# The mixture's weights two steps later in branch A's head loop, and the mixture in three places of a step

## The chip, the cores and the metric

The kernel runs on one core of one Trainium2 chip. The metric is the device time of one execution in microseconds (us). The core has five engines that run side by side, each in the order of its own instructions: PE (TensorE, matmuls), DVE (VectorE), ACT (ScalarE), POOL (GpSimd) and SP (SyncE, which here only issues DMAs). They wait for each other by semaphores, which the tile framework places. An engine whose next instruction waits does nothing of what stands behind it.

## The reference

One encoder layer over 1280 rows (1024 of a sample, 256 of a prompt) of width 1024: RMS norm, one wide projection, two attention branches side by side, gates, an output projection, an MLP with squared ReLU, a final norm. The branches are what matters here.

```python
o_a, _ = _banded_attention(qa, ka, va, A_WINDOW, 1, rel_bias[:, :A_HEADS], sink)
o_b = _dilated_mixture(qb, kb, vb, rel_bias[:, A_HEADS:])
merged = gates[:, :, 0] * (o_a.reshape(b, S, A_Q) @ w_branch_a) + gates[:, :, 1] * (o_b @ w_branch_b)
```

Branch A has 8 heads with a window of 128. Branch B has three groups of 4 heads with dilations 1, 4 and 16. Each group gives an output and, for every row and head, the log-sum-exp of its logits. The mixture weighs the three groups:

```python
alpha = jax.nn.softmax(jnp.stack(lses), axis=0)
o = jnp.sum(alpha[..., None] * jnp.stack(outs).astype(jnp.float32), axis=0)
```

## The kernel before

The kernel goes through its stages one after the other: norm and values, projections with branch B's attention beside the last of them, branch A's attention (about 552 to 710 us of the profile), gates and output projection, MLP up, MLP down. Float32 products are made of three matmuls of split operands (high and low parts), so PE is busy nearly all the time. In the stages that matter here the order of each engine's instructions is the order in which the Python code issues them; no scheduler changes it. Buffers come from pools: the pool `w` has 10 of 4 KB a partition, and the mixture's tiles `r`, the split weights `whi` and `wlo`, raw weights and the gate logits `gs` all come from it.

**The head loop** (lines 1336 to 1371). Branch A's heads are taken two at a time (a head pair u of 4), and each pair has 10 tiles of 128 rows. The list `order` holds the 40 (u, t). One step of the loop takes two tiles, so j runs over 0, 2, ..., 40, and the stages of a tile are spread over steps. In a step j stand, in this order:

1. scores of tile j on PE (L1093, L1094); DVE adds the bias and takes the maximum (L1095), and makes the negated maximum (`nm_a`, L1099); a piece of the fill; exponentials on ACT (L1105);
2. values of the tiles j-4 and j-3 on PE (L1132), the output copy on DVE (L1135, called the output copy in what follows) and its store by POOL's DMA queue (L1136);
3. **first place of the mixture** (L1345); a piece of the fill;
4. transposes of tile j-2's probabilities on PE (L1117), copied out of PSUM by ACT (L273) and, where the tile has three blocks, also by DVE (L275);
5. scores of tile j+1 and a piece of the fill;
6. transposes of tile j-1 with their copies; **second place of the mixture** (L1357); exponentials of tile j+1.

PE's *fill* is the generator `logits` (L1146): the gates' plain projections, cut into pieces of 4 or 8 matmuls. For each new column block the loop also splits a weight tile (ACT L231, DVE L235). At the steps with t = 0, SP loads the next head pair's queries (and keys for every second pair) and POOL loads its bias (L458), behind the step's other work.

**The mixture** is the generator `merge` (L1175). A call `next(merges)` runs it to its next `yield`. It holds:

- ahead of the loop: the maxima and sums of branch B (`nm_b`, `l_b`) are turned by PE, copied by DVE (L1182), written to DRAM by 13 small DMAs of POOL's queue (`scr_n`, L1187) and read back in another arrangement by 12 (L1204);
- first call in the loop: DVE copies the re-read parts into one order (L1209), takes the minimum over the groups and the differences (L1214 to L1216); ACT takes the exponential (L1217);
- second call: DVE sums, inverts and multiplies (L1219 to L1232), POOL's queue stores the weights (`scr_c`, 6 DMAs, L1235);
- third call: the load of item 0;
- then 18 items (three column blocks, two head pairs, three groups), two calls each: one loads the next item (`r`: branch B's outputs, L1250, and the weights spread over 64 partitions, two DMAs, L1253, all of POOL's queue) and multiplies this one on POOL (L1267); the other adds the product to `merged` on DVE (L1271), which groups 1 and 2 need and group 0 does not.

With two places a step from step 4 on, the first call comes behind the output copy of step 4, the second at the end of step 4, the products of items 0, 1, 2, ... at the ends of steps 6, 8, 10, ..., and each add at the output copy two steps later. The last item is left for `run(merges)` behind the loop (L1375). `merged` of the first column block is read in step 36 (`high_b`, `low_b`).

The functions that the diff touches, with the lines of the profile:

Of the kernel before, what the change touches and what calls it, by code (L numbers as in the profile page):

```python
# [97 lines left out]
def encoder_kernel(  # L98
# [120 lines left out]
    def fetch():  # L219
        src, shape, _ = specs[len(raws)]  # L220
        raws.append(wslot("raw", shape))
        nc.sync.dma_start(raws[-1], src)
# [200 lines left out]
    def load_unit(u):  # L423

        st = {}
        g = u // 2
        if u == 0:
            shared["kp"] = slot("kp", (P, 4, NP), F32R)
        if u % 2 == 0:
            kk = [slot("kk", (P, NS), F32R) for _ in range(2)]  # L430
            for i in range(2):
                for r in HALVES:
                    nc.sync.dma_start(kk[i][r, :].bitcast(F32), scr_ka[g, i, :, :NS])
                    nc.sync.dma_start(shared["kp"][r, 2 * g + i, :].bitcast(F32), scr_ka[g, i, :, NS:])
            shared["k"] = [Pair(kk[i], shared["kp"][:, 2 * g + i, :]) for i in range(2)]
        st["q"] = [Pair(slot("q", (P, NS), F32R), None) for _ in range(2)]
        for h in range(2):
            nc.sync.dma_start(st["q"][h].s.bitcast(F32), scr_qa[u][h].rearrange("a d t -> (a d) t")[:, :NS])
        if u:
            load_prompt(u, st)  # L440
        else:
            shared["v"] = [slot("va", (P, 8, P)), None]
            nc.sync.dma_start(shared["v"][0],
                              scr_v[:NS, 512 : 512 + P].rearrange("(t p) c -> p t c", p=P))
        st["k"], st["v"] = shared["k"], shared["v"]
        return st
# [9 lines left out]
    def load_bias(u, make):  # L456
        b = make("bias", (P, 2, 3 * P))
        nc.gpsimd.dma_start(b, toeplitz(0, 3 * P, -P, 2 * u))  # L458
        return b
# [611 lines left out]
    if True:  # L1071
# [3 lines left out]
        def a3(name, shape=(P, 2, 3 * P), n=3, dt=F32):  # L1075
            return att.tile(list(shape), dt, name=name, tag=name, bufs=n)
# [8 lines left out]
        def scores(u, t):  # L1085
            st, bias = units[u]
            lo, W, c0 = tiles[t]
            s = a3("s", n=3)
            m = small.tile([P, 2], F32, name="m", tag="m")
            for h in range(2):  # L1090
                ps = bank("sc")
                q = st["q"][h][:, P * t : P * t + P]
                nc.tensor.matmul(ps[:, :W], q, st["k"][1][:, P * lo : P * lo + W], start=True, stop=False)  # L1093
                nc.tensor.matmul(ps[:, :W], q, st["k"][0][:, P * lo : P * lo + W], start=False, stop=True)  # L1094
                nc.vector.tensor_tensor_reduce(  # L1095
                    s[:, h, :W], ps[:, :W], bias[:, h, c0 : c0 + W], 1.0, -3.0e38,
                    op0=ALU.add, op1=ALU.max, accum_out=m[:, h : h + 1],
                )
            nc.vector.scalar_tensor_tensor(nm_a[:, 2 * u : 2 * u + 2, t], m, -1.0, nsink[:, 2 * u : 2 * u + 2],  # L1099
                                           op0=ALU.mult, op1=ALU.min)  # L1100
            live[u, t] = s

        def exponential(u, t, h):
            W, s = tiles[t][1], live[u, t]
            nc.scalar.activation(s[:, h, :W], s[:, h, :W], AF.Exp, bias=nm_a[:, 2 * u + h : 2 * u + h + 1, t],  # L1105
                                 accum_out=l_a[:, 2 * u + h : 2 * u + h + 1, t])

        def transposes(u, t):

            W = tiles[t][1]  # L1110
            s = live[u, t]
            pt = a3("pt", (P, 6, P), 2)
            jobs = [(b, h) for b in range(W // P) for h in range(2)]
            for i, eng in ((0, nc.scalar), (4, nc.vector))[: 1 + (len(jobs) > 4)]:
                ps, e = bank("pt"), min(len(jobs), i + 4)
                for k, (b, h) in enumerate(jobs[i:e]):
                    nc.tensor.transpose(ps[:, P * k : P * k + P], s[:, h, P * b : P * b + P], ident)  # L1117
                moved(eng, pt[:, i:e, :], ps[:, : P * (e - i)].rearrange("p (i q) -> p i q", q=P))
            live[u, t] = pt

        def values_of(u, t):

            pv = bank("pv")
            for i in range(2):
                lo, W, _ = tiles[t + i]
                pt = live.pop((u, t + i))
                v, rest = units[u][0]["v"]
                for b in range(W // P):
                    k = lo + b
                    src = v[:, k, HALVES[u // 2]] if k < 8 else rest[:, k - 8, HALVES[u // 2]]  # L1130
                    for h in range(2):
                        nc.tensor.matmul(pv[HALVES[h], P * i : P * i + P], src, pt[:, 2 * b + h, :],  # L1132
                                         start=b == 0, stop=b == W // P - 1, skip_group_check=True)
            o = a3("o", (P, 2, P), 2)
            nc.vector.tensor_copy(o, pv[:, : 2 * P].rearrange("p (i q) -> p i q", i=2))  # L1135
            nc.gpsimd.dma_start(scr_o[t // 2][:, u], o)  # L1136
# [31 lines left out]
        def spread(src, g, b, x=0):  # L1168

            base, length, stride, R = place(g, b)  # L1170
            a = src[:, :]
            n = length // 32
            return bass.AP(a.tensor, a.offset + ROWS * P * x + base, [[n, P], [stride, R], [1, n]])

        def merge():  # L1175
# [23 lines left out]
            for g in range(3):  # L1199
                for b, sl in ((0, slice(0, 32)), (2, slice(32, 40))):  # L1200
                    R = place(g, b)[3]
                    for x in range(2):
                        dst = (raw[:, g, x, sl] if g else nat[:, x, 0, sl]).rearrange("p (r j) -> p r j", r=R)
                        nc.gpsimd.dma_start(dst, spread(scr_n, g, b, x))  # L1204
            yield
            for g in (1, 2):
                for b, sl in ((0, slice(0, 32)), (2, slice(32, 40))):
                    R = place(g, b)[3]
# [67 lines left out]
    if True:  # L1276
# [5 lines left out]
        def high_b(b):  # L1282

            ob_hi.block(b)
            ob_lo.block(b)
            nc.scalar.activation(ob_hi.t[b, 0], merged[b], AF.Copy)

        def low_b(b):
            nc.vector.tensor_tensor(ob_lo.t[b, 0], merged[b], ob_hi.t[b, 0].bitcast(F32), op=ALU.subtract)
# [3 lines left out]
        def load_o(t):  # L1293
            if t % 2 == 0:
                rows_o[t] = slot("o", (P, 4, 2, P))
                nc.sync.dma_start(rows_o[t], scr_o[t // 2])
# [34 lines left out]
        n = len(order)  # L1331
        fill = logits()
        merges = merge()
        next(merges)
        steps_of(fill, 2)
        for j in range(0, n + 2, 2):
            if j < n:
                scores(*order[j])
                next(fill)
                for h in range(2):  # L1340
                    exponential(*order[j], h)
            if j > 2:
                values_of(*order[j - 4])
                if j < n:
                    next(merges, None)  # L1345
            next(fill)
            if j:
                transposes(*order[j - 2])
            if j == n:
                next(fill)  # L1350
            if j < n:
                scores(*order[j + 1])
                next(fill)
            if j:
                transposes(*order[j - 1])
                if j > 2:
                    next(merges, None)  # L1357
            if j < n:
                for h in range(2):
                    exponential(*order[j + 1], h)  # L1360
            if j == n - 4:
                high_b(0)
                low_b(0)
            if j < n and order[j][1] == 0 and order[j][0] < 3:
                u = order[j][0] + 1
                units[u] = load_unit(u), load_bias(u, lambda name, shape: a3(name, shape, 2))
            if j in (n - 6, n - 4):
                fetch()
            if j == n - 2:
                load_o(0)  # L1370
                load_o(1)
# [573 lines left out]
```

## Time and profile before

| | us |
|---|---|
| median of 3 runs | 1724.98 |
| lowest and highest of the 3 | 1723.02, 1725.82 |
| the profiled execution | 1727.48 |
| its span, first to last instruction | 1725.3 |

The profile shows one execution. A row of a timeline has the start and the duration in us, the engine, the line, the operation, the tiles it writes and reads, the shapes and the count; in brackets stands how long the engine was idle ahead of it and what released it. DMA-issuing instructions stand on the engine that issues them, with the time of the issue; the landing comes later. A row of waits names who waited for whom, the total in us, how often, and the longest. A row of the windows gives a stretch, its length, the busy time (and number of instructions) of PE, PE's weight loads, DVE, ACT and POOL, then the granted clock of PE as a share of the full one, the DMA engines' share and GB/s.

### The profile page before, as it was taken

The page shows a single profiled execution, that of the slowest core. Times are in us where ns is not written, and L with a number is a line of the kernel's source. Part 1 is how long each engine was busy: PE and PEld are TensorE (multiplying, and loading weights), DVE is VectorE, ACT ScalarE, POOL GpSimd, SP SyncE. Part 2 cuts the span into 40 slices and gives each one's busy share as a digit, 9 for nine tenths or more (in the row PEclk, how much of TensorE's full clock was granted, in tenths as well). Part 3 has the DMA queues.
Part 4 walks back from the last instruction along what each step waited for, and adds up shares of the span by engine and source line. Part 5 has one row for each costly group of instructions (what it writes and reads, how often), then busy time and mean ns, then how long its engine had stood idle before and what let it go on. Part 6 is the DMA issues. An engine that isn't in the chain of part 4 may idle for free.

```text
span 1725.3 us, 24932 instructions
## 1 busy us (share of the span) xinstructions
PE 1682.3 (98%) x9230; PEld 1413.3 (82%) x9230; DVE 965.1 (56%) x1565; ACT 718.8 (42%) x1485; POOL 527.6 (31%) x451
## 2 busy tenths in 40 slices
PE   7999999999999799999999999999998999999998
PEld 6898888877778688888887888888887888888886
DVE  6733323445553466577368445454547776667575
ACT  6232222355553456654076333333334333333344
POOL 0212222212122664300100455555546242304140
PEclk9999999999999899999999999999999999999999
DMA  6414343576666574655021334433446835533333
GB/s 238 145 43 138 117 136 95 150 195 191 181 187 200 143 231 134 225 194 215 25 82 65 140 119 139 156 125 114 151 155 227 293 123 164 207 116 116 116 116 122
DMA packets 212424, 260.23 MB, mean 151 GB/s; under 512 B 21959, under 2 KB 141835, under 8 KB 212176
## 3 DMA queue, kind: packets, MB, share of 16 engines
q1 hardware_dynamic: 200704, 228.26, 40.1%
q0 software_dynamic: 10512, 28.29, 5.4%
q10 hardware_dynamic: 1088, 2.10, 0.4%
q8 instruction: 73, 1.20, 0.3%
q14 instruction: 47, 0.39, 0.1%
HBM read 173.03 MB, written 90.80 MB: 153 GB/s over the span
## 4 chain that ended last, share of the span: by engine, by line
PE 85%; issue 8%; DMA 2%; DVE 2%; POOL 1%; ACT 1%; SPq 0%; POOLq 0%; DVEq 0%; ACTq 0%
PE dn L355 21%; PE x L355 18%; PE mm L192 10%; PE z L355 9%; PE v L761 6%; PE mm L355 5%; PE pv L355 5%; PE y L355 4%; PE sc L538 2%; PE pv L581 1%; PE pt L568 1%; PE pv L1132 1%; DMA r<-scr_c 1%; PE pt L1117 1%; DMA scr_n<-cb 1%
## 5 line engine op out<-in xcount | busy, mean ns | idle before, releaser
L355 PE MATMUL dn<-dhi,ulo 128*128 128x512 f32 x448 | 175.3, 391 | 6.1 <-DVE ulo L186 6.1
L355 PE MATMUL dn<-dlo,uhi 128*128 128x512 f32 x448 | 175.0, 391 | 0.0
L355 PE MATMUL dn<-dhi,uhi 128*128 128x512 f32 x448 | 175.0, 391 | 0.0
L355 PE MATMUL x<-chi,wlo 128*128 128x512 f32 x424 | 167.6, 395 | 2.1 <-DVE u L1818 1.4
L355 PE MATMUL x<-clo,whi 128*128 128x512 f32 x424 | 165.8, 391 | 0.1
L355 PE MATMUL x<-chi,whi 128*128 128x512 f32 x424 | 165.1, 389 | 0.0
L322 DVE TENSOR_TENSOR wlo<-ta,whi 128x1024 fp32r<-128x1024 f32 x30 | 55.4, 1846 | 184.1 <-ACT whi L320 177.2
L322 DVE TENSOR_TENSOR wlo<-raw,whi 128x1024 fp32r<-128x1024 f32 x60 | 92.2, 1537 | 101.5 <-ACT whi L320 101.5
L397 POOL TENSOR_TENSOR tb<-raw 128x512 f32<-128x512 f32 x25 | 33.6, 1344 | 330.4 <-DMA raw<-in_w_in_dram 119.7
L355 PEld LDWEIGHTS dn<-dhi,ulo 128*128 128x128 f32 x448 | 84.6, 189 | 24.6 <-DVE ulo L186 7.0
L186 DVE TENSOR_TENSOR ulo<-uraw,uhi 128x1024 fp32r<-128x1024 f32 x56 | 93.9, 1695 | 13.5 <-ACT uhi L185 13.5
L355 PEld LDWEIGHTS dn<-dlo,uhi 128*128 128x128 f32 x448 | 84.5, 189 | 17.6
L355 PEld LDWEIGHTS dn<-dhi,uhi 128*128 128x128 f32 x448 | 84.5, 189 | 17.5
L355 PEld LDWEIGHTS x<-chi,wlo 128*128 128x128 f32 x424 | 79.7, 188 | 20.5 <-issue 3.1
L355 PEld LDWEIGHTS x<-chi,whi 128*128 128x128 f32 x424 | 79.6, 188 | 17.2
L355 PEld LDWEIGHTS x<-clo,whi 128*128 128x128 f32 x424 | 79.8, 188 | 14.8 <-DVE clo L322 0.4
L1643 POOL TENSOR_TENSOR t<-raw,t 128x1024 f32<-128x1024 f32 x16 | 45.4, 2854 | 149.5 <-DMA raw<-in_w_down_dram 138.6
L1794 DVE TENSOR_TENSOR v<-v,dn 128x512 f32<-128x512 f32 x90 | 59.6, 682 | 42.3 <-PE dn L355 41.3
L1890 POOL TENSOR_TENSOR u<-u,u 128x640 f32<-128x640 f32 x16 | 26.0, 1628 | 170.9 <-ACT u L1815 170.9
L558 ACT ACTIVATE s<-s,nm_b 128x128 f32<-128x128 f32 (+1 forms) x120 | 51.9, 434 | 54.5 <-DVE nm_b L550 54.5
L355 PE MATMUL pv<-phi,wlo 128*128 128x256 f32 x256 | 72.5, 283 | 1.7 <-ACT u L1814 1.7
L355 PE MATMUL dn<-dhi,up 128*128 128x512 f32 x224 | 73.5, 389 | 0.0
(312 smaller groups left out, 4676.3 us busy)
## 6 DMA issues: line engine op xcount, KB each, us to landing
scr_u<-u SPq DMA_DIRECT2D x112, 320.0 KB, 2.5
uraw<-scr_u SPq DMA_DIRECT2D x56, 512.0 KB, 4.0
raw<-in_w_in_dram SPq DMA_DIRECT2D x33, 512.0 KB, 5.5
raw<-in_w_up_dram SPq DMA_DIRECT2D x32, 512.0 KB, 4.8
raw<-in_w_down_dram SPq DMA_DIRECT2D x28, 512.0 KB, 6.3
sg<-scr_g SPq DMA_DIRECT2D x32, 256.0 KB, 5.9
uraw<-scr_u SPq DMA_DIRECT2D x28, 256.0 KB, 4.3
v<-scr_v SPq DMA_DIRECT2D x96, 64.0 KB, 2.5
```

The source lines that it names most:

```text
L186: nc.vector.tensor_tensor(lo, src, hi.bitcast(F32), op=ALU.subtract)
L192: nc.tensor.matmul(ps, a, b, start=i == 0, stop=i == len(seq) - 1)
L322: nc.vector.tensor_tensor(lo, src, hi.bitcast(F32), op=ALU.subtract)
L355: nc.tensor.matmul(ps, a, b, start=first and i == 0, stop=last and i == len(seq) - 1, skip_group_check=True)
L397: (nc.vector if vector else nc.gpsimd).tensor_tensor(o, x, y, op=ALU.subtract)
L538: nc.tensor.matmul(at(k, h)[p0 : p0 + nq, :], qk[rows, p0 : p0 + nq], qk[rows, P + P * a : P + P * a + W], start=True, stop=True, skip_gro ...
L558: nc.scalar.activation(s[:, h, :W], s[:, h, :W], AF.Exp, bias=nm[:, h : h + 1], accum_out=l[:, h : h + 1])
L568: nc.tensor.transpose(ps[:, P * a : P * a + P], s[:, h, P * k : P * k + P], ident)
L761: nc.tensor.matmul(ps[:, :n], a, b, start=k == 0 and j == 0, stop=k == KC - 1 and j == 2)
L1643: nc.gpsimd.tensor_tensor(o, a, b, op=ALU.subtract)
L1794: nc.vector.tensor_tensor(v, v, ps, op=ALU.add)
L1890: nc.gpsimd.tensor_tensor(u[S1], u21, u22, op=ALU.add)
```

## The change

Two edits. In `merge`, behind the reads of the statistics, five calls pass instead of one before the generator goes on. With two calls a step these are four more, so the first call's work (L1209 to L1217) comes behind the output copy of step 8 instead of step 4, and the weights (L1219 to L1235) at the end of step 8. In the loop, from step 10 on a third call stands between the two: behind the scores of tile j+1 and their piece of the fill, ahead of the transposes of tile j-1.

```diff
@@ merge
                         nc.gpsimd.dma_start(dst, spread(scr_n, g, b, x))
-            yield
+            for _ in range(5):
+                yield
             for g in (1, 2):
@@ head loop
             if j < n:
                 scores(*order[j + 1])
                 next(fill)
+                if j >= 10:
+                    next(merges, None)
             if j:
                 transposes(*order[j - 1])
                 if j > 2:
                     next(merges, None)
```

The calls then fall like this: item 0 is loaded at the output copy of step 10 and multiplied in its middle place; item 1 is multiplied at the output copy of step 12 and added in its middle place; item 2 is multiplied at the end of step 12 and added at the output copy of step 14; three items in two steps from there on, the last add at the output copy of step 34. No instruction is added or left out. The orders of PE and SP stay the same; on ACT the one exponential moves; on DVE and POOL the mixture's operations and DMAs move past the others.

## The prediction

> **What bounds the kernel now.** I read the page first, then the waits of the stage that the diff touches (545 to 730 us), then DVE's, POOL's and PE's timelines in it.
>
> ```profile
> span 1725.3 us, 24932 instructions
> ...
> PE 1682.3 (98%) x9230; PEld 1413.3 (82%) x9230; DVE 965.1 (56%) x1565; ACT 718.8 (42%) x1485; POOL 527.6 (31%) x451
> ```
>
> PE is busy 98% of the span, and its order of instructions is the same in the changed kernel, as is SP's. So the end can only move by what PE idles, or by what its clock loses behind an idle time. The waits of the stage name one such place:
>
> ```profile
> ACT cb L1217 <- DVE cb L1216: 12.2, 1, 12.2
> PE pt L1117 <- ACT pt L273: 11.1, 1, 11.1
> DVE cb L1209 <- DMA cb<-scr_n: 10.5, 4, 6.7
> ...
> DVE merged L1271 <- POOL r L1267: 4.8, 2, 3.1
> ...
> PE sc L1093 <- DVE m L1095: 1.3, 1, 1.3
> ```
>
> Read from below: DVE's copies of the re-read statistics (L1209) wait for their DMAs; ACT's exponential (L1217) waits for DVE; behind it ACT holds back a copy of transposed probabilities, and PE stands 11.1 us. The last two rows are a smaller stall: an add of the mixture (L1271) waits for POOL's product, the next scores' reduction comes late, PE waits 1.3. How much of the stage is lost shows in the output copy (L1135), which stands once in each step; I call its start in step j O(j). It reaches O(4) = 566.62.
>
> ```profile
> 566.62 0.42 DVE L1135 COPY o<-pv 128x256 f32<-128x256 f32 x1 [1.21 <-PE pv L1132]
> ...
> 578.18 0.17 DVE L1209 COPY cb<-cb 128x16 f32<-128x16 f32 x1 [0.39 <-DMA cb<-scr_n]
> ...
> 578.73 0.28 DVE L1216 TENSOR_TENSOR cb<-cb 128x120 f32<-128x120 f32 x1
> ...
> 587.65 0.42 DVE L1135 COPY o<-pv 128x256 f32<-128x256 f32 x1 [1.18 <-PE pv L1132]
> ...
> 615.87 0.42 DVE L1135 COPY o<-pv 128x256 f32<-128x256 f32 x1 [0.16 <-PE pv L1132]
> ...
> 623.99 0.42 DVE L1135 COPY o<-pv 128x256 f32<-128x256 f32 x1 [1.43 <-PE pv L1132]
> ```
>
> ```profile
> 630.70 0.42 DVE L1135 COPY o<-pv 128x256 f32<-128x256 f32 x1 [1.22 <-PE pv L1132]
> ...
> 643.28 0.42 DVE L1135 COPY o<-pv 128x256 f32<-128x256 f32 x1 [0.56 <-PE pv L1132]
> ...
> 650.06 0.42 DVE L1135 COPY o<-pv 128x256 f32<-128x256 f32 x1 [1.07 <-PE pv L1132]
> ...
> 657.28 0.42 DVE L1135 COPY o<-pv 128x256 f32<-128x256 f32 x1 [1.10 <-PE pv L1132]
> ```
>
> These are O(4), O(6), O(14), O(16), then O(18), O(22), O(24), O(26). A head pair has ten tiles, so the work of a step repeats every five steps. From O(16) to O(26) PE runs without a gap: five steps take 33.29 us, the one from 24 to 26 takes 7.22. The same five steps from O(4) to O(14) take 49.25, which is 15.96 too long (the first one alone 21.03 against 7.22, 13.8 too long), and the step from 14 to 16 takes 8.12, 0.90 too long. **All that can be won here is 16.9 us.**
>
> **The change, part by part.**
>
> *The weights two steps later.* DVE's copies and ACT's exponential come behind O(8) instead of O(4). Undisturbed, O(8) is 566.62 + 7.22 + 6.71 (623.99 to 630.70) = 580.55. Everything ahead of the stall is unchanged, so the last re-read lands before 578.18, as now: 2.4 us of margin, and the 11.1 us wait goes. The small operations stay, and now run beside a busy PE:
>
> ```profile
> 583.55 0.27 DVE L1219 TENSOR_TENSOR cb<-cb 128x120 f32<-128x120 f32 x1
> ...
> 584.88 0.45 DVE L1232 TENSOR_TENSOR cb<-cb 128x32 f32<-128x32 f32 x4
> ...
> 594.35 0.42 DVE L1135 COPY o<-pv 128x256 f32<-128x256 f32 x1 [1.50 <-PE pv L1132]
> ...
> 597.33 1.20 DVE L1099 SCALAR_TENSOR_TENSOR nm_a<-m,nsink 128x2 f32<-128x2 f32 x1
> ...
> 610.95 1.04 DVE L1271 TENSOR_TENSOR merged<-merged,r 128x512 f32<-128x512 f32 x1 [3.13 <-POOL r L1267]
> ```
>
> The second group takes 1.7 us (583.55 to 585.25, when POOL goes on, below), the first about 1.6 (the four copies and three operations at some 0.2 each). DVE stands idle 1.1 to 1.5 us ahead of most output copies (the rows above), so most of each group is covered by that slack. I take 0.3; the bounds are 0 and 3.3, both groups without cover. No gain is possible there, since nothing waits for them earlier than now.
>
> *What is late next.* The weights themselves come out no earlier. DVE does: O(8) 580.55, output copy 0.42, first group 1.6, a probability copy and two reductions of 0.4 each, second group 1.7: 585.7, where it was 585.25 before. POOL's chain hangs on that:
>
> ```profile
> 576.74 0.72 POOL L458 DMA_DIRECT2D bias<-wide  x1
> ...
> 585.25 4.14 POOL L1235 DMA_DIRECT2D scr_c<-cb  x6 [7.21 <-DVE cb L1232]
> ...
> 597.24 1.27 POOL L1267 TENSOR_TENSOR merged<-r 128x512 f32<-128x512 f32 x1 [3.26 <-DMA r<-scr_c]
> 598.47 0.60 POOL L1136 DMA_DIRECT2D scr_o<-o  x1
> 599.07 0.90 POOL L1250 DMA_DIRECT2D r<-scr_b  x1
> 599.95 1.37 POOL L1253 DMA_DIRECT2D r<-scr_c  x2
> 601.34 1.30 POOL L1267 TENSOR_TENSOR r<-r 128x512 f32<-128x512 f32 x1
> ```
>
> Six stores of the weights, the output store, two loads of 1.6 to 2.3 us, the wait for the first to land, the first product. So that product ends at 598.5 + 0.4. In the changed order a bias load (0.7), an output store (0.6), a third load (0.90 + 1.37) and then the second product (1.3) follow: 603.8. But the loop is no longer held up. The second product's add now stands in step 12, in the new middle place, behind the second tile's scores (about 3 us after the output copy: 597.33 against 594.35). O(12) is O(14) less 6.78 (643.28 to 650.06); O(14) is 566.62 + 33.29 = 599.91, with the 0.3 above 600.2. So DVE arrives at about 596.5 and stands until 603.8, adds (1.04) and only then copies the transposed tile (0.42): 605.3. PE needs that copy for the last matmuls of step 14's values, just ahead of O(14), at 599.8. **It stands 5.5 us.** The bounds are 2.2 (the first load has landed when POOL asks for it: 3.26 less) and 9.
>
> An idle PE comes back slower:
>
> ```profile
> 585.00:587.50 2.50, 2.50 (x27) 1.70 (x25) 1.44 (x9) 0.91 (x3) 2.25 (x4) 0.76 0.04 8
> 1330.00:1332.50 2.50, 0.00 (x0) 0.00 (x0) 2.50 (x1) 0.88 (x2) 2.50 (x2) 0.56 0.20 78
> ...
> 1335.00:1337.50 2.50, 2.50 (x8) 1.88 (x7) 2.50 (x3) 1.06 (x1) 2.50 (x2) 0.57 0.66 262
> ```
>
> ```profile
> 1333.13 0.79 PE L355 MATMUL dn<-dhi,ulo 128*128 128x512 f32 x1 [5.36 <-DVE ulo L186]
> ```
>
> The number behind the busy times is the granted clock. After the 5.36 us idle it is 0.57 on average from 1335 to 1337.5, so at half until 1337.15, 4.0 us after PE's return; after the 11.1 us idle it was back at 586.2. A wait of 5.5 is nearest to the former: 4.0 us at half speed, **2.0 us**. Bounds: 0, if the wait is too short for the clock to fall, and 2.6.
> [...]
>
> *The mixture in three places.* Each of the 18 loads and products stays; 12 adds on DVE stay. From step 12 on three calls a step instead of two: of two steps, the first has one product in the middle place, the second a product at the output copy, its add in the middle, and a third product at the end, whose add stands behind the next output copy. Behind a waiting add DVE holds the probability copy and the next reduction, and PE waits for those; behind a waiting product POOL holds output stores and bias loads. For what a late add costs there are two cases now. The landing times are those of the loads r from 640 to 660 and from 590 to 605:
>
> ```profile
> DMA to landing us min/median/max: 3.1/4.2/4.5
> ```
>
> ```profile
> DMA to landing us min/median/max: 6.0/7.9/10.0
> ```
>
> The add at 610.95 ended 4.6 us behind O(12), and its step lasted 1.7 longer than its fellow (615.87 - 607.39 = 8.48 against 6.78):
>
> ```profile
> 607.39 0.42 DVE L1135 COPY o<-pv 128x256 f32<-128x256 f32 x1 [1.08 <-PE pv L1132]
> ```
>
> In step 14 the third add waits for a load of the pressed time; its product ends some 1.5 us behind O(14), its add some 3: I take 0.8, bounds 0 and 1.7. From step 16 on the loads land in 4.2. In the second step of a pair the output copy (0.4), store (0.6), load (2.27) and product (1.3) put the product 4.6 us behind O, the add to 5.7, the copy to 6.1; PE needs it about 6.2 behind O, at the next values. So it just fits. The end product waits for a load issued 3.7 us earlier, ends 8 us behind O, and its add 2.4 behind the next O: covered too. I take 0.2 for each of five pairs, **1.0**; bounds 0 and 6.
>
> *The end.* The last product and add come in step 34, no longer behind the loop. PE has its fill there and did not wait for them: 0.
>
> **Sum:** 16.9 - 0.3 - 5.5 - 2.0 - 0.8 - 1.0 = 7.3 us. The profiled execution took 1727.48, 2.2 around its span; it becomes 1720.2. The median shown, 1724.98, lies 2.5 below that execution; I take the 7.3 off it: **1717.7**.
>
> **The rivals.**
>
> [...]
> 2. *The denser products eat it.* A small DVE operation (L1099, m and nsink) took 1.20 us at 597.33, beside the product at 597.24:
>
> ```profile
> L1099 DVE SCALAR_TENSOR_TENSOR nm_a<-m,nsink 128x2 f32<-128x2 f32 x40 | 15.0, 376 | 1.4
> ```
>
>    It averages 0.376 over 40, so about eight of them are held 1.1 longer. With the products nearer to the reductions ten more may be held; if half of that (5.5) reaches PE, the gain is 1.8: 1723.2. In its favour are the tight 6.1 against 6.2.
>    [...]
> 3. *Slower: the loads land late.* If each load takes the 7.9 us of the pressed stretch, in five pairs the end product's add comes 3.7 later, all of it on PE: 7.3 - 18.5 = -11.2, 1736.2. It decides from a landing time of about 5.7 (1.5 more in each pair). Against it stands the 4.2 of the calmer stretch; for it, that half as many loads again fall into each step.
> 4. *It does not do what it says.* The last re-read lands behind O(8), and the first wait stays in part: from 582 on each microsecond counts, and with 4 of them the gain is 3.3: 1721.7. Nothing ahead of it changes, so this is the least likely.
>
> **How the numbers follow.** Forecast 0.58, rivals 0.12, 0.18, 0.08, 0.04. About 0.2% (3.4 us) is what a measurement of this kernel can tell from no change. Faster: nearly all of the forecast, rival 1, a little of 2 and 4: 0.74. Same: most of 2, the rest of the forecast and 4: 0.17. Slower: 0.09. The range reaches from rival 1 to rival 2, 1712.4 to 1723.5; outside lie rival 3 and the edges of the others.
>
> **What would show it.** In the changed profile PE's wait for ACT's copy (11.1) is gone, and the weights' stores on POOL start at about 585.7. In step 12 the second add waits some 7 us for POOL, with PE idle near 600 and a granted clock of 0.5 behind it; O(16) lies near 615.7 instead of 623.99, and from there the steps last 6.3 to 7.2. I am wrong if no add waits in step 12, if steps behind 16 are longer than their fellows, or if DVE's copies of the statistics still wait for DMAs.

## The result, and the profile after

The changed kernel is slower: 1730.09 us in the median of 8 runs (1727.70 to 1732.45), against 1725.46 of the kernel before in 8 runs beside it (1723.02 to 1727.01). The ratio is 1.0028, with a 95% interval of 1.0017 to 1.0039. The forecast was 1717.7, so the sum is 12.4 us out and has the wrong sign. The profiled execution of the changed kernel took 1730.95. All lines of `merge` behind the diff's first edit carry numbers higher by one than in the kernel before (L1272 was L1271).

From the page:

```profile
span 1729.1 us, 24928 instructions
...
PE 1685.5 (97%) x9230; PEld 1415.2 (82%) x9230; DVE 962.7 (56%) x1565; ACT 717.9 (42%) x1485; POOL 526.1 (30%) x451
```

The span is 3.8 longer. From the waits of the stage (545 to 730 us: who waits for whom, total, times, longest):

```profile
DVE merged L1272 <- POOL r L1268: 24.6, 9, 12.0
...
POOL r L1268 <- DMA r<-scr_c: 9.1, 7, 2.5
...
PE pv L1132 <- DVE pt L275: 10.2, 1, 10.2
...
POOL merged L1268 <- DMA r<-scr_c: 5.0, 1, 5.0
PE sc L1093 <- DVE m L1095: 2.9, 2, 1.4
```

The 11.1 us of before (PE for ACT's copy) is gone. In its place stands one of 10.2, and behind it a new kind of row: DVE's adds wait nine times for POOL's products (4.8 us in all before), and these wait eight times for their loads. POOL's and DVE's timelines show how the first of them comes about.

```profile
585.29 4.12 POOL L1236 DMA_DIRECT2D scr_c<-cb  x6 [3.07 <-DVE cb L1233]
...
591.90 0.53 POOL L1254 DMA_DIRECT2D r<-scr_c  x1 [0.81 <-DMA scr_c<-cb]
593.50 0.78 POOL L1251 DMA_DIRECT2D r<-scr_b  x1 [1.07 <-ACT s L1105]
594.99 0.63 POOL L1254 DMA_DIRECT2D r<-scr_c  x1 [0.71 <-DMA scr_c<-cb]
596.11 0.62 POOL L1254 DMA_DIRECT2D r<-scr_c  x1 [0.48 <-DMA scr_c<-cb]
601.74 1.25 POOL L1268 TENSOR_TENSOR merged<-r 128x512 f32<-128x512 f32 x1 [5.01 <-DMA r<-scr_c]
...
606.54 1.27 POOL L1268 TENSOR_TENSOR r<-r 128x512 f32<-128x512 f32 x1
```

```profile
565.98 0.42 DVE L1135 COPY o<-pv 128x256 f32<-128x256 f32 x1 [1.21 <-PE pv L1132]
...
607.85 1.03 DVE L1272 TENSOR_TENSOR merged<-merged,r 128x512 f32<-128x512 f32 x1 [12.02 <-POOL r L1268]
611.30 0.41 DVE L1135 COPY o<-pv 128x256 f32<-128x256 f32 x1
...
614.05 2.95 DVE L235 TENSOR_TENSOR wlo<-raw,whi 128x1024 fp32r<-128x1024 f32 x1 [1.36 <-ACT whi L231]
...
621.39 0.42 DVE L1135 COPY o<-pv 128x256 f32<-128x256 f32 x1 [1.44 <-PE pv L1132]
...
642.34 1.04 DVE L1272 TENSOR_TENSOR merged<-merged,r 128x512 f32<-128x512 f32 x1 [4.46 <-POOL r L1268]
...
661.10 0.42 DVE L1135 COPY o<-pv 128x256 f32<-128x256 f32 x1
```

The output copies are O(4), O(14), O(16) and O(26). The weights' stores start at 585.29, where 585.7 was forecast, but the second product ends at 607.81 and not at 603.8. O(4) to O(16) takes 55.41 (57.37 before, 49.1 forecast); O(16) to O(26) takes 39.71 (33.29 before). So the change wins 2.0 us up to O(16) and then loses 6.4.

### The profile page after: what moved, and what is told of

Same layout as the page of the kernel before. It is cut to its first block, busy times and chain, and to the rows that moved or that the text cites. A ratio compares the mean times of both kernels' runs of the same rounds, so it can differ in the third digit from the quotient of the medians.

```text
span 1729.1 us, 24928 instructions
## 1 busy us (share of the span) xinstructions
PE 1685.5 (97%) x9230; PEld 1415.2 (82%) x9230; DVE 962.7 (56%) x1565; ACT 717.9 (42%) x1485; POOL 526.1 (30%) x451
## 4 chain that ended last, share of the span: by engine, by line
PE 85%; DVE 5%; DMA 3%; issue 2%; ACT 2%; POOL 2%; POOLq 0%; SPq 0%; DVEq 0%; ACTq 0%
PE dn L355 21%; PE x L355 18%; PE mm L192 12%; PE z L355 9%; PE v L761 5%; PE mm L355 5%; PE pv L355 5%; PE y L355 4%; PE sc L538 2%; PE pv L581 1%; PE pt L568 1%; DMA r<-scr_c 1%; PE pv L1132 1%; PE tr L346 1%; DMA scr_n<-cb 1%
```

## The experiments

Each kernel below computes the whole layer. The table gives, for the profiled execution of each, stretches between the output copies of the steps (differences of the starts in DVE's timeline). Without any hold-up the three take 33.29, 7.22 and 33.29 (worked out in the prediction from the kernel before); what one step loses the next can in part win back, so that a kernel with 8.17 in the second comes to 32.19 in the third. A profile is one execution, and in three kernels it lies about 3 us beside the median: 1731.97 (two pairs' loads later), 1713.56 (add later, third place from 10) and 1722.13 (loads two items ahead).

| kernel | median us | ratio to before, 95% | O(4) to O(14) | to O(16) | to O(26) |
|---|---|---|---|---|---|
| before | 1725.46 | | 49.25 | 8.12 | 33.29 |
| the change | 1730.09 | 1.0017 to 1.0039 | 45.32 | 10.09 | 39.71 |
| first edit alone | 1722.18 | 0.9971 to 0.9990 | 33.22 | 17.97 | 33.67 |
| second edit alone | 1740.40 | 1.0076 to 1.0117 | 52.40 | 9.13 | 41.14 |
| third place from step 24 | 1722.81 | 0.9973 to 0.9992 | 33.68 | 17.11 | 33.67 |
| two pairs' loads later | 1728.55 | 1.0007 to 1.0030 | 39.31 | 10.10 | 42.97 |
| add later, third place from 24 | 1712.31 | 0.9908 to 0.9933 | 33.25 | 8.17 | 32.19 |
| add later, third place from 10 | 1716.42 | 0.9933 to 0.9963 | 33.22 | 8.18 | 34.54 |
| loads two items ahead | 1725.05 | 0.9989 to 1.0009 | 43.34 | 9.38 | 35.03 |
| add later, loads two ahead | 1715.66 | 0.9932 to 0.9956 | 33.46 | 8.96 | 38.68 |
| the same, step 22 without its first place | 1716.38 | 0.9933 to 0.9960 | 33.29 | 11.13 | 34.99 |
| fourth pair's loads later | 1731.52 | 1.0022 to 1.0050 | 45.26 | 11.66 | 36.39 |
| first edit, add later | 1720.21 | 0.9964 to 0.9984 | 33.22 | 8.68 | 31.68 |

The theory to be tested: the two edits have separate costs. The first one takes the old wait away, but the weights come no earlier, so the second product's add makes DVE and PE wait again. The second edit brings load, product and add so close together that any load that lands late is passed on to PE. The rival: it is the add in the middle place that makes the first wait, so that the first edit alone has none.

**The first edit alone.**

```diff
-                if j >= 10:
-                    next(merges, None)
```

> The first edit alone: weights at step 8, two places a step, so the second product's add stands at the output copy of step 14. Theory 'late chain' (the first loads of the mixture land beside the third head pair's loads, the second product ends near 608 wherever its add stands): DVE waits 7 to 9 us ahead of that add, PE idles 5 to 8 us with the clock at half behind it, 1719 to 1724 with the tail that is left behind the loop. Rival 'middle place' (the add asked for too early in step 12 is what costs): no wait over 2 us, PE's stretch from the output copy of step 4 to that of step 16 takes 42 us or less, 1711 to 1716.

1722.18 us. Its waits:

```profile
DVE merged L1272 <- POOL r L1268: 14.7, 3, 8.7
...
PE pt L1117 <- DVE pt L275: 7.9, 1, 7.9
```

The wait is there without the middle place, two places later and only 2.3 us shorter: the rival falls. Behind O(16) the steps are nearly as they were before (33.67 and 33.29). So the second edit costs the other 8 us.

**The second edit alone.**

```diff
-            for _ in range(5):
-                yield
+            yield
```

> The second edit alone: the weights at step 4 as before, the third place from step 10 on. The 11 us wait for the statistics must be back. Theory 'density costs by itself' (the 6 us that steps 16 to 26 lost in the changed kernel): 1729 to 1733. Rival 'density costs only where the chain is late and loads press': 1724 to 1727, steps behind 16 as before.

1740.40 us, 14.7 above the kernel before (1725.73 in that series): more than either expectation allowed. The old wait is back, and its other rows are the dense ones:

```profile
DVE merged L1271 <- POOL r L1267: 20.0, 8, 5.8
PE pt L1117 <- ACT pt L273: 13.2, 3, 11.0
POOL r L1267 <- DMA r<-scr_c: 7.9, 5, 4.6
PE sc L1093 <- DVE m L1095: 6.7, 5, 3.3
```

Eight adds wait, five products wait for their loads, and PE stands 6.7 us in five places behind them; before, that last row had 1.3. Three places are dear without the first edit too.

**The third place only from step 24.**

```diff
-                if j >= 10:
+                if j >= 24:
```

> Both edits, but the third place only from step 24 on, behind the fourth head pair's loads. Up to step 24 it equals the first edit alone, and nothing is left behind the loop. Late chain: 1718 to 1723, steps 16 to 24 at 6.3 to 6.8 us each. Middle place: 1710 to 1715. If density costs everywhere, steps 24 to 38 are 0.5 or more longer each than in the kernel before.

1722.81 us: the same as the first edit alone within the intervals, with 7.97 us of PE behind the first add (7.92 there). The third place is not free behind step 24: O(26) to O(36) takes 35.21, and 33.32 with the first edit alone. But the three items that are otherwise left for behind the loop are gone, and the rest of the span, from O(36) on, is 1.6 shorter. So it wins nothing while the first add's wait stays.

**The loads of the third and fourth head pair two steps later.** SP's timeline of the changed kernel:

```profile
584.14 0.70 SPq L433 DMA_DIRECT2D kk<-scr_ka  x1
...
591.38 0.83 SPq L451 DMA_DIRECT2D qp<-scr_qa  x2
```

The third pair's keys and queries are issued from 584.14 to 592.2, and the mixture's first loads from 589.98 to 596.7. In the kernel before, SP's came later, from 595.45 to 605.2.

```diff
-            if j < n and order[j][1] == 0 and order[j][0] < 3:
+            if j < n and order[j][1] == (4 if order[j][0] else 0) and order[j][0] < 3:
```

> Both edits, and the loads of the third and fourth head pairs (queries, keys, bias) two steps later, in steps 14 and 24, away from the mixture's first loads. Late chain by pressed landing: the first product starts at 597 to 598 instead of 601.7, DVE waits 7 to 8 us instead of 12.0, PE idles 5 to 6 us instead of 10.2, and the time is 1722 to 1726. Rival 'POOL's own issue time': DVE's wait stays over 10.5 us and the time at 1729 to 1731.

1728.55 us, above the 1722 to 1726 expected. The first product started at 598.64 instead of 601.74, and the first wait shrank by nearly half:

```profile
DVE merged L1272 <- POOL r L1268: 18.5, 8, 6.8
...
PE pv L1132 <- DVE pt L275: 4.9, 1, 4.9
```

6.75 for DVE and 4.93 for PE are nearly the 7.3 and 5.5 of the prediction: with SP's loads out of the way, its working holds. (The third pair's bias load, 0.75 us of POOL, left the chain with them; without it the working would say 6.6 and 4.8.) The landing times say the same. From 589 to 600, the changed kernel's loads:

```profile
r<-scr_b POOLq DMA_DIRECT2D x2, 256.0 KB, 9.8
r<-scr_c POOLq DMA_DIRECT2D x4, 128.0 KB, 8.9
```

and those of this kernel (the last column is the median from issue to landing):

```profile
r<-scr_b POOLq DMA_DIRECT2D x2, 256.0 KB, 6.8
r<-scr_c POOLq DMA_DIRECT2D x4, 128.0 KB, 6.3
```

But SP's loads, now at 609.08 to 618.5, meet the mixture's next ones. The add at 629.58 waits 5.04, PE 4.09, and O(16) to O(26) grows to 42.97. Of the 6.0 us won up to O(14), the median keeps 1.5, and the intervals of the two kernels overlap.

**The first add four places later, the third place from step 24.** If the theory holds, nothing should wait when the add stands where its product has long been done.

```diff
                 yield
+                if k == 1:
+                    for _ in range(4):
+                        yield
                 if g:
...
-                if j >= 10:
+                if j >= 24:
```

> The weights two steps later, the first add of the mixture four places behind its product's own next place (O(18) rather than O(14)), everything behind it as much later, two places a step up to step 22 and three from 24 on. The theory (the first edit takes PE's 11.1 us wait away and the second product's add puts it back as 8 to 10 us, clock included): the first add finds its product long done, no PE wait between O(4) and O(18) above 1 us, O(14) to O(16) at 7 to 8.1 instead of 17.1, and the time 10 us below the kernel with the third place from step 24 only (1722.8): 1711 to 1714. The rival (the wait only moves on to the next late load or product): a wait of 4 us or more shows at the first add or the two behind it, and the time is 1718 to 1723.

1712.31 us, 13.0 below the kernel before and 17.8 below the changed one: the best version here. The windows from 560 to 670 (PE busy stands first, and the granted clock third from the end) show what was won. The kernel before:

```profile
560.00:670.00 110.00, 97.15 (x760) 81.73 (x758) 62.04 (x197) 57.30 (x156) 64.76 (x89) 0.94 0.61 179
```

The change:

```profile
560.00:670.00 110.00, 94.76 (x717) 79.43 (x716) 59.53 (x187) 52.82 (x147) 67.37 (x94) 0.92 0.60 172
```

This kernel:

```profile
560.00:670.00 110.00, 109.91 (x882) 94.45 (x880) 67.66 (x222) 65.73 (x180) 67.88 (x95) 1.00 0.63 183
```

PE is busy in 109.91 of 110 us at the full clock, against 94.76 at 0.92. O(4) to O(26) takes 73.61, where the kernel before takes 90.66: 17.05 less. The prediction's "all that can be won here is 16.9" was right for this stretch. The median wins 13.0 of it: from O(26) to O(36), where the third place now stands, this kernel takes 35.97 against 33.22.

**The same with the third place from step 10** (six places later, which is two whole steps):

```diff
+                if k == 1:
+                    for _ in range(6):
+                        yield
```

> The changed kernel with the first add, and all that stands behind it, two steps (six places) later; three places a step from step 10 on. If the first add's wait and the later losses are separate terms, the 10.2 us wait of PE and its half clock go and the later 6 us stay (loads that land late in three places, with the fourth pair's loads of SP from step 20 on): 1717 to 1720, with steps behind 20 still longer than their fellows. If the late add only set off the later losses (everything shifted against SP's loads), they go too: 1711 to 1714. If three places cost as much as they did without the first edit (14.7 us over the stage), 1724 to 1728.

1716.42 us (1713.56 to 1720.87), between two of the expectations. The profile shows the shortest of the six executions. In it the first wait is gone, and the later losses went with it for the larger part: O(14) to O(26) takes 42.72, 2.2 more than the undisturbed 40.51, where the change takes 49.80. But three executions took 1713.6 to 1714.3 and three 1718.5 to 1720.9, and the longer ones have no profile; in those the later losses may be there as before. So it is not shown that the late first add set them off. What differs in the profile: in the changed kernel the fourth pair's queries are issued at 632.33, 4.0 us ahead of the next load of POOL (636.31), here at 614.37, 6.1 us ahead of it (620.46). That this is the reason is argued from one profile of each.

**Each load two items ahead of its product.**

```diff
             load(0)
+            load(1)
             yield
...
-                load(k + 1)
+                load(k + 2)
```

> The changed kernel with each item's load issued two items ahead of its product instead of one; products, adds and places stay. If the three places lose their time because a load has only two places (3.7 to 6 us) to land in, the products behind step 14 wait for no DMA, the steps from 16 to 26 come back to 33.3 to 35 (39.7 in the changed kernel), and the time is 1723 to 1726; the first add still waits 10 us or more. If it is POOL's products that hold DVE, or POOL's own issue time, the steps stay near 39 and the time is 1729 to 1732.

1725.05 us, 5.0 below the change. O(16) to O(26) comes back from 39.71 to 35.03 (in an execution of 1722.13; the twelve range from 1721.20 to 1729.73). The waits that are left:

```profile
DVE merged L1273 <- DMA r<-scr_b: 10.1, 1, 10.1
PE pv L1132 <- DVE pt L275: 8.5, 1, 8.5
...
DVE merged L1273 <- POOL r L1269: 1.9, 1, 1.9
```

One add waits for a product behind the first one, where it was eight. The products and adds are in the same places as in the changed kernel, so in this execution most of the later loss (4.7 of 6.4) was landing time.

**Add later and loads two ahead together.** The edits of the last two kernels in one:

```diff
+            load(1)
...
-                load(k + 1)
+                load(k + 2)
...
+                if k == 1:
+                    for _ in range(6):
+                        yield
```

> Both of the two before: the first add two steps later, and the loads two items ahead. If late landing and the late first add are all that the change costs, nothing waits and the time is 1710 to 1713, the best of all kernels here. If three places a step cost POOL's or DVE's time by themselves, 1717 to 1721.

1715.66 us: a miss. Nothing waits at the first add, but the step from O(24) to O(26) takes 11.46. DVE's timeline there:

```profile
638.47 3.71 DVE L235 TENSOR_TENSOR wlo<-raw,whi 128x1024 fp32r<-128x1024 f32 x1 [1.87 <-ACT whi L231]
```

The split of a gate weight takes 1.23 in every other place of this kernel. Here POOL multiplies from 639.12 to 640.40. PE stands 2.59 behind it, and the granted clock is 0.50 from 642.5 to 645.

**The same without the first place of step 22**, which puts all that stands behind it one place later. It was to keep POOL's loads and products away from that split:

```diff
-                if j < n:
+                if j < n and j != 22:
                     next(merges, None)
```

> The kernel with the first add two steps later and loads two items ahead, with the first place of step 22 left out (everything behind it comes one place later), so that POOL issues no load and no product there while DVE makes the low half of a gate weight (L235). In the kernel it is taken from, that split lasted 3.71 us beside POOL's product and load issues (1.23 elsewhere), PE stood 2.6 and the clock fell to half, and the step from 22 to 24 took 11.5. If POOL's work held the split: it lasts 1.2 to 1.4, the step takes 6.8 to 7.5, and the time is 1711 to 1713.5. If the split is long there for another reason: 3.7 again, and 1715 to 1717.

```profile
640.83 1.23 DVE L235 TENSOR_TENSOR wlo<-raw,whi 128x1024 fp32r<-128x1024 f32 x1 [1.70 <-ACT whi L231]
```

The split is back at 1.23 and the step from O(24) to O(26) at 7.73. But the edit does not keep POOL's work away:

```profile
641.71 1.48 POOL L1269 TENSOR_TENSOR r<-r 128x512 f32<-128x512 f32 x1
```

POOL runs ahead of its places. Its product still begins within the split, 0.88 us behind the split's start instead of 0.65, with load issues beside it as before (640.09 to 641.69), and now it is the product that is a little longer (1.48 instead of 1.28). So the edit only shifted the two against each other. That POOL's work held the split in the kernel before is read from that kernel's rows, and not shown by a run without it.

The time is no better, 1716.38, because other steps lost about as much in this execution. The split at 604.27 waits 3.53 us for POOL's first product, PE stands 1.76 there, and O(14) to O(16) takes 11.13 (2.92, 1.17 and 8.96 in the kernel that it is taken from); O(26) to O(36) is 1.0 longer, too. With loads one item ahead (the kernel with the add later and the third place from step 10) the split does not wait for that product.

**The fourth head pair's loads at step 24**, the third pair's in their place.

```diff
+            if j < n and order[j][1] == (4 if order[j][0] == 2 else 0) and order[j][0] < 3:
```

> The changed kernel with the fourth head pair's queries and bias loaded at step 24 instead of step 20; the third pair's stay. If SP's loads are what makes the mixture's loads land late behind step 18: the stretch from O(16) to O(26) falls from 39.7 to 35 or 36, the rest stays (first add's wait 10 to 12), and the time is 1725 to 1727.5. If the moved loads only meet the mixture some steps later: as long a stretch is lost, and 1729 to 1731.

1731.52 us: right in the stretch, wrong in the time. The loads of the mixture from 620 to 640 in the changed kernel, and SP's loads of queries beside them:

```profile
r<-scr_c POOLq DMA_DIRECT2D x8, 128.0 KB, 5.5
q<-scr_qa SPq DMA_DIRECT2D x2, 512.0 KB, 8.7
```

and in this one, which has no loads of queries there:

```profile
r<-scr_c POOLq DMA_DIRECT2D x8, 128.0 KB, 3.6
```

O(16) to O(26) falls to 36.39. But then SP's loads come at 652.90, the mixture's weights land in 5.3 to 5.9 from 640 to 660, and the two steps from 24 to 28 lose 1.7 and 2.0. Another 1.6 goes between O(14) and O(16), where PE stands 2.17 behind the split (1.10 in the change) and the clock falls to half once more (0.50 from 620 to 622.5). The moved loads met the mixture again.

**The first edit with the add later, and no third place at all.**

```diff
+                if k == 1:
+                    for _ in range(4):
+                        yield
...
-                if j >= 10:
-                    next(merges, None)
```

> The first edit alone with the first add four places later: two places a step throughout, five items left for behind the loop. Nothing waits inside the loop: from O(4) to O(26) as with the third place from step 24 (73.0). If the third place is needed to get the last items out of the way, the five items behind the loop cost PE 5 to 10 us and the time is 1717 to 1722; if PE's work there covers them, 1711 to 1713 and the second edit is worth nothing.

1720.21 us. No wait inside the loop, but the last five items are left for behind it:

```profile
706.25 1.33 PE L1318 MATMUL pt<-ident,wl 128*128 128x128 f32 x5 [5.13 <-POOL wl L1308]
```

POOL copies `wl` for the next stage only when it is through with the items. So the third place is worth 7.9 us (1720.21 to 1712.31, two series with the kernel before at 1725.09 and 1725.33), if it starts late.

## Why the prediction was wrong

Two terms of the sum were too small, both because the mixture's loads land later than they did in the kernel before (in the median 9.8 and 8.9 us from 589 to 600, where 7.1 and 6.3 were measured before, and 5.5 for the weights from 620 to 640, where it was 4.5): PE's wait behind the second product's add (5.5 us, 10.2 measured), and the three places from step 16 on (1.0 us, 6.4 measured up to O(26)). The clock behind the wait adds 1.0.

*Right.* The old wait went, and the last re-read landed in time; the weights' stores started at 585.29 (585.7 forecast, though the terms named for it add up to 585.5); the small operations cost next to nothing (O(4) to O(12) takes 26.58 against 26.51 undisturbed). The second product's add in step 12 became the next late thing, with PE idle near 600 (10.20 up to 609.27) and half clock behind it (0.50 from 610 to 615). The end cost nothing: from O(36) on the steps are the same. What could be won, 16.9, was right, too. One of the prediction's own signs of being wrong came true: steps behind 16 are longer than their fellows.

*Wrong: "It stands 5.5 us".* PE stood 10.2. The mechanism was right and the size wrong, by one row. The prediction took POOL's wait for the first load from the kernel before (3.26). But SP's loads of the third pair, which now start ahead of the mixture's first loads (584.14 and 589.98), landed beside them: the wait was 5.01 (the row at 601.74), and the loads' own waits for the weights' landing and for ACT pushed their issue back by some 3 us (0.81, 1.07, 0.71 and 0.48; 0.36 in all in the kernel before). The first product ended at 602.99 and not at 598.9, the second 4.0 later than forecast; the other 0.7 is that PE ran dry at 599.07 and not at 599.8. The kernel with SP's loads moved away brings PE's wait to 4.93. These loads come earlier once the old wait is gone, and the sum did not ask what they still have in flight when the mixture's start.

*Wrong: the clock, 2.0 us.* From PE's timeline and the windows:

```profile
609.27 0.70 PE L1132 MATMUL pv<-pt,va 128*64 128x128 f32 x4 [10.20 <-DVE pt L275]
```

```profile
610.00:612.50 2.50, 2.50 (x8) 2.01 (x9) 2.46 (x5) 1.00 (x3) 1.76 (x2) 0.50 0.34 125
612.50:615.00 2.50, 2.50 (x10) 2.40 (x9) 1.14 (x2) 2.00 (x5) 2.48 (x5) 0.50 0.39 129
615.00:617.50 2.50, 1.40 (x8) 0.93 (x8) 2.50 (x3) 0.60 (x1) 0.91 (x1) 0.95 0.58 186
```

0.95 in the last window leaves 0.25 us at half, so the full clock came back at 615.25, 6.0 us after PE's return and not 4.0: 3.0 us instead of 2.0. That size is one execution's, and partly luck. In the kernel with the fourth pair's loads later PE comes back at 609.40 from a wait of 9.99, and the full clock 3.05 us after it:

```profile
610.00:612.50 2.50, 2.50 (x10) 1.99 (x9) 2.47 (x5) 0.84 (x3) 1.60 (x2) 0.51 0.41 146
```

Half of 6.0 and half of 3.05, 3.0 and 1.5 us, lie on either side of the 2.0. The range's lower end, 1712.4, takes the second wait at 2.2 and nothing for the clock (16.9 - 0.3 - 2.2 - 0.8 - 1.0 = 12.6). No run shows a wait of 2.2 that leaves the clock alone. In that same kernel PE stands 2.17 up to 617.54, and soon after it the clock is at half:

```profile
620.00:622.50 2.50, 2.50 (x22) 2.02 (x22) 0.11 (x1) 1.31 (x4) 0.00 (x0) 0.50 0.02 7
```

*Wrong: the third add in step 14, 0.8.* It did not wait at all. The step from O(14) to O(16) lost 2.87 over 7.22 all the same: 2.0 by the half clock up to 615.25, and PE's 1.1 idle behind the split that took 2.95 (614.05) beside POOL's product:

```profile
614.61 1.29 POOL L1268 TENSOR_TENSOR merged<-r 128x512 f32<-128x512 f32 x1
```

That is the second rival's mechanism, on another instruction than the one it named: L1099 took 12.3 us in its 40, less than the 15.0 of the kernel before. In the two kernels with the same schedule but without a middle place at step 14 that split takes 1.21 and 1.22 (first edit alone, and third place from 24); in the three that share the place it takes 2.94 to 2.96. Where the product began 0.23 us later within the split (step 22's place left out), 3.71 became 1.23.

*Wrong: "so it just fits", 1.0.* From O(16) to O(26) alone 6.4 are lost, where five pairs were given 0.2 each. The prediction saw that copy and need lay 0.1 us apart (6.1 against 6.2), and that the sum turns negative from a landing time of about 5.7. Then it took the calm landing time (4.2) for all pairs. From 620 to 640, beside the fourth pair's queries, the weights' loads took 5.5 in the median; the product behind O(20) waited 2.45 for one, the add of the row at 642.34 waited 4.46, and PE stood three times. This is the third rival, but mostly in one pair (the steps behind O(20) and O(22) lose 3.1 and 2.5) and not in five. That it is landing time is shown by two runs: loads two items ahead, with products and adds in place, give 35.03, and the fourth pair's loads elsewhere 36.39, with landing at 3.6.

The account up to O(16): 55.41 - 49.1 = 6.3 over the forecast. Behind it: 39.71 - 33.29 = 6.4, and 0.8 from O(26) to O(36) (34.01 against 33.22), less the 1.0 that was forecast, 6.2. Together 12.5, and the median differs from the forecast by 12.4. That these agree so well is luck: the profiled execution is only 10.8 over the 1720.2 forecast for it. It reached O(4) 0.6 earlier than the kernel before, and won 0.8 behind O(36).

*Not settled:* whether three places from step 10 on really lose less behind O(14) when the first add stands two steps later (the shortest execution shows it, the longer ones have no profile), and why; and how much of the second edit's own 14.7 is landing and how much is DVE held by POOL.

## What to carry to other kernels

When a wait is taken away, everything behind it moves up, also on queues that the change does not touch (here SP's loads of the third pair, from 595.45 to 584.14): look up which transfers of other queues start earlier, and price the landing of your own in their company rather than in that of the old trace (9.8 and 8.9 us beside those loads, 6.8 and 6.3 with them moved away). If a producer comes no earlier in absolute time, move its consumer back as well; here four places between the second product and its add were worth 10.5 us (1722.81 to 1712.31). Where the slack of a repeated step is 0.1 us, take the worst landing time for the range's other end and the forecast too, or buy the slack (a load one item further ahead brought 4.7 of 6.4 us back in the profiled execution, 5.0 in the median).

## What the runs showed of the hardware

In the cases below, POOL's product and DVE's split of a weight meet and at least one of the two takes longer than elsewhere; it can be either. Beside a product that began within it, the split took 2.95 instead of 1.23 (above), and ended 1.10 behind the product's end (617.00 and 615.90). In the kernel with the add later and the third place from step 10, the split begins at 600.50 and keeps its 1.23, and the product is stretched from 1.25 to 2.26:

```profile
600.61 2.26 POOL L1268 TENSOR_TENSOR merged<-r 128x512 f32<-128x512 f32 x1 [5.04 <-PE pt L1117]
```

In this second case the product ends about where it would if its 1.25 began only behind the split (600.50 + 1.23 + 1.25 = 602.98; it ended at 602.87). In the first case the split started first too, at 614.05, and was still the one that took longer. So which of the two starts first does not settle it. Up to 614.60 POOL issued a load. Whether that can hold the split is open: with the first edit alone the split ran beside such issues (610.34 to 611.93) in 1.21, but with loads two items ahead it began at 612.58, took 2.25, and the product beside it began only at 613.81, by when an undisturbed split would have been through.

The clock also fell behind three short gaps. In the changed kernel PE's gaps behind 642.5 were 1.43, 0.56 and 1.44 us, with PE busy 4.1 of the 7.5 us up to 650 (1.09, 1.82 and 1.18 in the three windows), and yet:

```profile
647.50:650.00 2.50, 1.18 (x4) 1.01 (x5) 2.46 (x8) 0.37 (x1) 2.50 (x5) 0.88 0.70 173
650.00:652.50 2.50, 2.50 (x15) 2.28 (x16) 1.76 (x5) 1.53 (x6) 1.75 (x2) 0.50 0.84 282
652.50:655.00 2.50, 2.50 (x26) 2.09 (x23) 0.96 (x2) 1.94 (x6) 0.60 (x2) 0.94 0.29 89
```

It was at half from about 649.4 (0.88 leaves 0.6 us) to 652.8 (0.94 leaves 0.3): 1.7 us lost, on top of the 3.4 of the gaps.
